# A decoder layer on one core: the second MLP product begins with four column tiles taken together, and units of its first chunk are loaded and split later

## The chip, the cores and the metric

The kernel runs on one core of one Trainium2 chip. The metric is the device time of one execution in microseconds (us); lower is better. Three runs of the kernel before are shown, and one more execution was taken with the hardware profiler. All stretches and times below are microseconds from the start of the profiled span.

## What is computed

One layer of a hybrid decoder on a residual stream of 512 positions and 2048 columns, in float32. The change touches only the MLP of the layer:

```
f = jnp.square(jax.nn.relu(rms_norm(h, norm_mlp_pre[i]) @ mlp_w1[i])) @ mlp_w2[i]
h = h + rms_norm(f, norm_mlp_post[i])
```

`mlp_w1` is 2048 by 8192 and `mlp_w2` is 8192 by 2048. Ahead of the MLP stand the recurrent and attention mixers and their output product, behind it a gate product with `ple_gate`.

## The kernel before

**Split products.** Every float32 operand is split into a rounded part (hi) and what is left (lo). ScalarE writes hi (line 155), VectorE writes lo from the source and hi (line 156), and one 128x128 weight block times one activation tile is three matmuls into the same PSUM bank (`mm3`, lines 163 to 165): hi with hi, hi with lo, lo with hi. A split activation tile of 128 contraction rows is a *unit* (hi and lo side by side). Units lie in two rings of buffers, `cx` with 14 and `cy` with 10.

**Strips.** The program of the second half of the layer is a list of *strips*. A strip is a piece of weights of 128 by 512, four blocks of 128x128, so it gives 12 matmuls. `go` walks the list; step j does three things in this order: it issues the work hooked to step j, it splits the weights of strip j+4, and it issues the matmuls of strip j, with the work hooked to the quarters of the step between them. `at(j, ...)` hooks work to a step (quarters are allowed). There are five buffers for split strips (tags `shi` and `slo`), so the split of strip j+4 waits until TensorE is through strip j-1. All orders are fixed by the numbers of the hooks; each engine and the DMA queue of SyncE take their instructions strictly in that order, and wait only where data or a buffer is missing.

**The first MLP product** (`mlp_w1`) ends in pairs of column tiles, each worked out with seven products instead of eight (`pair_a`, `add_pair`). A pair has 14 strips, and its matmuls have 256 columns of activations. Sums of weights for it lie in a ring of three buffers (tag `wsum`, 128x1024 each); the last pair holds two of the three, one until its tenth strip is split and one until its fourteenth. Weights as they arrive lie in a ring of five buffers (tag `raw`, 128x1024). The squared result goes to a DRAM tensor `f_d`.

**The second MLP product** (`mlp_w2`, in `back`, from the line `base = len(self.strips)`) is cut into 4 chunks of 16 units (2048 contraction rows each); every chunk goes over 16 column tiles, 4 strips each (`add_full`), and its matmuls have 512 columns. For each chunk, `load_f` (line 1506) brings two tiles of `f_d` at a time, 512 KB, into one `wsum` buffer, and `prep_b` splits one of them into a unit. For the first chunk, the loads and the splits are hooked to steps ahead of the first strip, `base`:

```
o = F0 + 0.5 * k if c == 0 else F1 + 4 * k if k < 8 else F2 + 0.4 * (k - 8)
if k % 2 == 0:
    at(cb + o - (4 if c == 0 or k < 14 else 0.5), load_f, c, k)
at(cb + o, prep_b, c, k)
```

With F0 = -11.75 the first load is hooked 15.75 steps ahead of the product, one more follows with every step, and the 16 splits are hooked from step base-11.75 to base-4.25, two to a step. The last pair of the first product is strips base-14 to base-1.

`add_plain` (line 242), which two other products of the layer use already, orders strips otherwise: it takes up to four column tiles together. Its first step issues the first strips of all four columns, block by block (for each block of 128 rows, the four columns in turn, 48 matmuls); then come the second strips of the four columns, the third and the fourth. Each column has a PSUM bank of its own.

Of the kernel before, what the change touches and what calls it, by code (L numbers as in the profile page):

```python
# [18 lines left out]
KT = D // P  # L19
# [11 lines left out]
FC = 16  # L31
NCHUNK = DFF // P // FC
FW = 10
F0, F1, F2 = -11.75, -48, -3
NTAB = 1039
H = S // 2
PRIO = 20000
# [1 line left out]
RMT = 11.5  # L39
WO = (-12, -11, -10, -9, -7, -5)  # L40
NPL = 6
NPG = 6
G6 = (-7, -6)
G4 = 21
# [91 lines left out]
class Build:  # L136
# [32 lines left out]
    def at(self, j, fn, *a):  # L169
        key = math.floor(4 * j + 0.5)  # L170
        assert self.now is None or key > self.now, (key, self.now)
        self.hooks.setdefault(key, []).append((fn, a))
# [1215 lines left out]
    def back(self):  # L1388
        nc, A, T, at = self.nc, self.A, self.T, self.at
# [55 lines left out]
        def plain_a(m0):  # L1445
            def f(i, ps, st):
                if i % 2 == 0:
                    st["z"] = x_tile()
                t = st["z"][:, i % 2]
                v.tensor_tensor(t, ps, T["Rm"], op=ALU.mult)  # L1450
                v.scalar_tensor_tensor(t, t, 0.0, t, op0=ALU.max, op1=ALU.mult)
                if i % 2:
                    self.store(self.f_d[m0 + i - 1:m0 + i + 1].rearrange("a p n -> p a n"), st["z"])
            return f

        def sink_a(m):
            def f(p, ps, st):
                z = self.z_evict(p, ps, st)
                if z is not None:
                    zf = z.rearrange("p a n -> p (a n)")  # L1460
                    v.scalar_tensor_tensor(zf, zf, 0.0, zf, op0=ALU.max, op1=ALU.mult)
                    self.store(self.f_d[m:m + 2].rearrange("a p n -> p a n"), z)
            return f
# [13 lines left out]
        self.add_plain(bk, [A["mlp_w1"][m] for m in range(4)], up, plain_a(0), "Rm", (-8.5, -7.5, -6.5, -5.5))  # L1477
        if NPL > 4:
            self.add_plain(bk + 16, [A["mlp_w1"][m] for m in range(4, NPL)], up, plain_a(4), "Rm", (-7, -6))
        for k in range(KT):  # L1480
# [9 lines left out]
        b = len(self.strips)  # L1490
        for m in range(NPL, DFF // P, 2):
            self.pair_a(b, A["mlp_w1"], m, ua, sink_a(m), first=m == NPL and NPL == 4, offs=WO if m == NPL and NPL > 4 else None, last=m == DFF // P - 2)
            b += 14
# [8 lines left out]
        ub = [[] for _ in range(NCHUNK)]  # L1502
# [15 lines left out]
        def out_b(c, m, ps):  # L1518
            y = self.y_row(m)
            if c == 0:  # L1520
                act.activation(y, ps, AF.Copy)
            else:
                v.tensor_tensor(y, ps, y, op=ALU.add)
            if c == NCHUNK - 1:
                sq = self.msum if m == 0 else self.sum_tile("fsq")[:, :S]
                act.activation(sq, y, AF.Square)  # L1526
                if m >= KT - 2:
                    sq_last.append(sq)
                elif m:
                    g.tensor_tensor(self.msum, self.msum, sq, op=ALU.add)  # L1530

        def add_full(c, m):
            q, st = {}, []
            b = len(self.strips)

            def load(h):
                q[h] = self.raw_tile()
                nc.sync.dma_start(q[h], A["mlp_w2"][c, m][:, h * 1024:(h + 1) * 1024])

            def mm(s):  # L1540
                def f(j, k):
                    if s + k == 0:
                        st.append(self.bank())
                    hi, lo = self.hl[j]
                    u = ub[c][4 * s + k]
                    self.mm3(st[0], hi[:, k * P:(k + 1) * P], lo[:, k * P:(k + 1) * P], u[:, 0], u[:, 1],
                             s + k == 0, s == 3 and k == 3)
                    if s == 3 and k == 3:
                        self.wait.append(("j", out_b, c, m, st[0]))
                return f  # L1550

            for h in range(2):
                at(b + 2 * h - FW, load, h)
            for s in range(4):
                self.strips.append(Strip(lambda s=s: q[s // 2][:, (s % 2) * 512:(s % 2 + 1) * 512], mm(s)))

# [2 lines left out]
        for c in range(NCHUNK):  # L1559
            cb = len(self.strips)  # L1560
            for k in range(FC):
                o = F0 + 0.5 * k if c == 0 else F1 + 4 * k if k < 8 else F2 + 0.4 * (k - 8)
                if k % 2 == 0:
                    at(cb + o - (4 if c == 0 or k < 14 else 0.5), load_f, c, k)
                at(cb + o, prep_b, c, k)
            for m in range(KT):
                add_full(c, m)


        last = len(self.strips)  # L1570
# [42 lines left out]
        def plain_g(i, ps, st, m0=0):  # L1613
            i += m0
            pp, h = T["ph", i - i % 2]
            o = pp[:, i % 2]
            t = T["fb"].tile([P, S], F32, tag="t2", name="og", bufs=1)
            act.activation(t, ps, AF.Sigmoid)
            g.tensor_tensor(o, o, t, op=ALU.mult)  # L1619
            g.tensor_tensor(o, o, h[:, i % 2], op=ALU.add)  # L1620
            if i % 2:
                self.store(self.out[:, i - 1:i + 1, :], pp, GD)

        def g_sink(m):
            def f(p, ps, st):
                z = self.z_evict(p, ps, st)
                if m < KT - 2:
                    parts = [(r, slice(0, S)) for r in range(2)] if z is not None else []
                else:
                    parts = self.done({2: 0, 7: 2}.get(p, p))  # L1630
                if not parts:
                    return
                (pp, h), zz = T["ph", m], st["z"]
                for r, c in parts:
                    o = zz[:, r, c]
                    act.activation(o, o, AF.Sigmoid)
                    v.tensor_tensor(o, o, pp[:, r, c], op=ALU.mult)
                    v.tensor_tensor(o, o, h[:, r, c], op=ALU.add)
                if m < KT - 2:
                    self.store(self.out[:, m:m + 2, :], z, 2)  # L1640
                elif p == 4:
                    nc.sync.dma_start(self.out[:, m + 1, :], zz[:, 1])
                elif p in (2, 3, 7):
                    nc.sync.dma_start(self.out[:, m, c], o)
            return f
# [14 lines left out]
        self.add_plain(bg, [A["ple_gate"][m] for m in range(4)], ug, plain_g, "Rf", (-12, -11, -10, -7))  # L1660
        if NPG > 4:
            self.add_plain(bg + 16, [A["ple_gate"][m] for m in range(4, NPG)], ug,
                           lambda i, ps, st: plain_g(i, ps, st, 4), "Rf", G6)
# [3 lines left out]
        at(bg + GL + 1, load_ph, 2)  # L1667
        for m in range(NPG, KT, 2):
            b = len(self.strips)
            self.pair_a(b, A["ple_gate"], m, ue, g_sink(m), last=m == KT - 2, offs=GO if m == NPG else None,  # L1670
                        lo=lambda p, m=m: g if p in GP and m == NPG else None)
            at(b + GH, load_ph, m)
# [99 lines left out]
```

## Time and profile before

| | |
|---|---|
| median of 3 runs | 2459.36 us (2458.16 to 2459.91) |
| the profiled execution | 2458.5 us, of which the span is 2456.7 us |
| instructions | 34978 |
| TensorE busy | 2342.9 us, 95% of the span |
| VectorE, ScalarE, GpSimd busy | 1544.3, 1076.8, 243.5 us |
| granted TensorE clock, mean | 0.979 |

In the profile, PE is TensorE's matmuls, DVE VectorE, ACT ScalarE, and SPq the DMA queue of SyncE. A row of a timeline begins with the start and the duration; what stands in brackets at its end is the idle time of that engine just before, and what ended it. A matmul's duration reaches past the start of the next one, so the spacing of starts is what it costs in a row of matmuls. Names lose their digits: `in_mlp_w_dram` is either of the two weight tensors.

### The profile page before, as it was taken

To read this page: it belongs to the slowest core of one execution; us is meant where nothing else is said; L and a number is where in the kernel's file an instruction comes from. 1 tells how busy PE (TensorE), PEld (TensorE's weight loads), DVE (VectorE), ACT (ScalarE), POOL (GpSimd) and SP (SyncE) were. 2 spreads that over 40 slices of the span, in tenths; PEclk is the share of its full clock that TensorE was granted. 3 is DMA by queue.
4 is the path that set the end of the run, shared out by engine and by line. 5 is a ranking of instruction groups with operands and counts; after the bars stand their busy time and mean duration, and the time that the engine had idled before them with its cause. 6 is when DMAs were issued, how large, how long until landed. Compare 5 with 4: busy or idle time off the path is not lost.

```text
span 2456.7 us, 34978 instructions
## 1 busy us (share of the span) xinstructions
PE 2342.9 (95%) x13178; PEld 2046.3 (83%) x13178; DVE 1544.3 (63%) x2543; ACT 1076.8 (44%) x2008; POOL 243.5 (10%) x238
## 2 busy tenths in 40 slices
PE   7999999989999778999999998999999999997899
PEld 6788888777788658999999997888888888886688
DVE  6364755588746789888888886333333333335898
ACT  5354655478733445444444444333223223223454
POOL 4000000134400440000000000000000000112420
PEclk9999999999999889999999999999999999998999
DMA  5452232422234532343433333434333333233644
GB/s 191 159 180 93 99 108 97 133 89 84 82 129 164 191 103 98 127 138 130 136 131 134 134 135 126 159 116 133 112 112 137 121 103 131 101 112 128 223 142 138
DMA packets 114093, 316.75 MB, mean 129 GB/s; under 512 B 11298, under 2 KB 16674, under 8 KB 113924
## 3 DMA queue, kind: packets, MB, share of 16 engines
q1 hardware_dynamic: 94708, 275.13, 34.0%
q10 hardware_dynamic: 19216, 39.39, 4.2%
q8 instruction: 103, 1.69, 0.3%
q14 instruction: 66, 0.54, 0.1%
HBM read 270.37 MB, written 44.11 MB: 128 GB/s over the span
## 4 chain that ended last, share of the span: by engine, by line
PE 62%; DVE 6%; issue 2%; DMA 1%; ACT 1%; POOL 0%; ACTq 0%; DVEq 0%; SPq 0%; POOLq 0%
PE ps_mm L165 20%; PE ps_mm L163 20%; PE ps_mm L164 20%; DVE slo L156 1%; DVE cx L156 1%; DMA fk<-f_d 1%; DVE y L1592 1%; PE ps_t L487 0%; DVE y L442 0%; POOL pz L1619 0%; ACT shi L155 0%; DVE y L1422 0%; DVE cy L156 0%; DVE y L1588 0%; DMA pz<-pp_d 0%
## 5 line engine op out<-in xcount | busy, mean ns | idle before, releaser
L156 DVE TENSOR_TENSOR slo<-raw,shi 128x512 fp32r<-128x512 f32 x802 | 580.0, 729 | 743.1 <-ACT shi L155 727.4
L155 ACT ACTIVATE shi<-raw 128x512 fp32r<-128x512 f32 x804 | 502.2, 629 | 870.5 <-PE ps_mm L164 748.4
L163 PE MATMUL ps_mm<-cx,shi 128*128 128x512 f32 (+1 forms) x2044 | 707.7, 346 | 25.4 <-ACT shi L155 19.8
L164 PE MATMUL ps_mm<-cx,shi 128*128 128x512 f32 (+1 forms) x2044 | 702.1, 343 | 15.0 <-DVE cx L1428 7.5
L165 PE MATMUL ps_mm<-cx,slo 128*128 128x512 f32 (+1 forms) x2044 | 704.0, 344 | 13.0 <-DVE slo L156 10.7
L165 PE MATMUL ps_mm<-cy,slo 128*128 128x512 f32 (+1 forms) x1604 | 555.0, 346 | 6.4 <-DVE slo L156 6.4
L163 PE MATMUL ps_mm<-cy,shi 128*128 128x512 f32 (+1 forms) x1604 | 555.4, 346 | 3.7 <-ACT shi L155 2.0
L164 PE MATMUL ps_mm<-cy,shi 128*128 128x512 f32 (+1 forms) x1604 | 554.9, 346 | 4.1 <-DVE cy L1428 4.1
L163 PEld LDWEIGHTS ps_mm<-cx,shi 128*128 128x128 f32 x2044 | 393.0, 192 | 70.8 <-ACT shi L155 23.5
L165 PEld LDWEIGHTS ps_mm<-cx,slo 128*128 128x128 f32 x2044 | 392.5, 192 | 62.7 <-DVE slo L156 16.6
L164 PEld LDWEIGHTS ps_mm<-cx,shi 128*128 128x128 f32 x2044 | 393.3, 192 | 57.8 <-DVE cx L1428 8.8
L165 PEld LDWEIGHTS ps_mm<-cy,slo 128*128 128x128 f32 x1604 | 305.8, 191 | 44.6 <-DVE slo L156 8.0
L163 PEld LDWEIGHTS ps_mm<-cy,shi 128*128 128x128 f32 x1604 | 305.9, 191 | 40.8 <-ACT shi L155 2.6
L164 PEld LDWEIGHTS ps_mm<-cy,shi 128*128 128x128 f32 x1604 | 305.9, 191 | 40.5 <-DVE cy L1428 4.8
L155 ACT ACTIVATE shi<-wsum 128x512 fp32r<-128x512 f32 x204 | 126.5, 628 | 163.9 <-PE ps_mm L164 87.8
L156 DVE TENSOR_TENSOR slo<-wsum,shi 128x512 fp32r<-128x512 f32 x204 | 138.7, 687 | 44.8 <-ACT shi L155 44.8
L1530 POOL TENSOR_TENSOR msum<-msum,fsq 128x512 f32<-128x512 f32 x13 | 16.9, 1297 | 1288.7 <-ACT fsq L1526 1288.7
L1257 POOL TENSOR_SCALAR al_P<-al_P,ar_sts 128x512 f32<-128x512 f32 (+3 forms) x128 | 74.2, 601 | 63.8 <-ACT al_ph L1279 29.3
L163 PE MATMUL ps_mm<-y,shi 128*128 128x256 f32 x272 | 76.4, 281 | 1.2 <-ACT shi L155 1.2
L1247 ACT ACTIVATE al_P<-al_P,ar_stm 128x512 f32<-128x512 f32 (+3 forms) x128 | 70.4, 554 | 16.1 <-DVE ar_stm L1242 15.8
L165 PE MATMUL ps_mm<-y,slo 128*128 128x256 f32 x272 | 76.1, 280 | 0.8 <-DVE slo L156 0.8
L164 PE MATMUL ps_mm<-y,shi 128*128 128x256 f32 x272 | 75.9, 279 | 0.0
(356 smaller groups left out, 2336.3 us busy)
## 6 DMA issues: line engine op xcount, KB each, us to landing
raw<-in_mlp_w_dram SPq DMA_DIRECT2D x254, 512.0 KB, 3.7
raw<-in_w_in_dram SPq DMA_DIRECT2D x64, 512.0 KB, 3.5
raw<-in_w_out_dram SPq DMA_DIRECT2D x32, 512.0 KB, 3.5
fk<-f_d SPq DMA_DIRECT2D x32, 512.0 KB, 5.0
raw<-in_ple_gate_dram SPq DMA_DIRECT2D x32, 512.0 KB, 4.8
f_d<-z ACTq DMA_DIRECT2D x29, 512.0 KB, 2.8
y<-in_xT_dram SPq DMA_DIRECT2D x16, 256.0 KB, 6.2
raw<-in_w_v_dram SPq DMA_DIRECT2D x8, 512.0 KB, 4.3
```

The source lines that it names most:

```text
L155: nc.scalar.activation(hi, src, AF.Copy)
L156: (eng or nc.vector).tensor_tensor(lo, src, f32(hi), op=ALU.subtract)
L163: mm(ps, whi, ahi, start=start, stop=False)
L164: mm(ps, whi, alo, start=False, stop=False)
L165: mm(ps, wlo, ahi, start=False, stop=stop)
L1247: act.activation(PP[qt, b], PP[qt, b], AF.Exp, scale=-1.0, bias=st["mn"][:, qt, b:b + 1], accum_out=st["sm"][:, qt, b:b + 1])
L1257: pool.tensor_scalar(PP[qt, b], PP[qt, b], st["sm"][:, qt, b:b + 1], 1.0, op0=ALU.mult, op1=ALU.mult)
L1530: g.tensor_tensor(self.msum, self.msum, sq, op=ALU.add)
L1592: v.scalar_tensor_tensor(y, y, V[:, V_MLPPOST + k:V_MLPPOST + k + 1], T["h"][k], op0=ALU.mult, op1=ALU.add)
```

## The change

The first four column tiles of the first chunk go through `add_plain` instead of `add_full`. Their first weight loads are hooked to steps base-12 to base-9. The times of the loads and splits of the first chunk's 16 units come from two tables, `CL` (8 loads) and `CU` (16 splits): loads from base-10 to base+5.25, splits from base-6 to base+8.5. The two columns behind the four load their weights 8 steps ahead instead of 10. Nothing else is changed; the arithmetic and the number of matmuls, splits and transfers are the same.

```
-F0, F1, F2 = -11.75, -48, -3
+F1, F2 = -48, -3
...
+CU = (-6, -4.75, -3.5, -2.25, -1, -0.5, 0.25, 0.75, 4.25, 4.75, 5.25, 5.75, 7, 7.5, 8, 8.5)
+CL = (-10, -7.5, -5, -2.75, 0.25, 0.75, 1.75, 5.25)
...
-        def add_full(c, m):
+        def add_full(c, m, lead):
...
-                at(b + 2 * h - FW, load, h)
+                at(b + 2 * h - lead, load, h)
...
-                o = F0 + 0.5 * k if c == 0 else F1 + 4 * k if k < 8 else F2 + 0.4 * (k - 8)
+                o = CU[k] if c == 0 else F1 + 4 * k if k < 8 else F2 + 0.4 * (k - 8)
                 if k % 2 == 0:
-                    at(cb + o - (4 if c == 0 or k < 14 else 0.5), load_f, c, k)
+                    at(cb + CL[k // 2] if c == 0 else cb + o - (4 if k < 14 else 0.5), load_f, c, k)
                 at(cb + o, prep_b, c, k)
-            for m in range(KT):
-                add_full(c, m)
+            if c == 0:
+                self.add_plain(cb, [A["mlp_w2"][c, m] for m in range(4)], ub[c], lambda i, ps, st: out_b(0, i, ps), "j",
+                               (-12, -11, -10, -9))
+            for m in range(4 if c == 0 else 0, KT):
+                add_full(c, m, 8 if c == 0 and m < 6 else FW)
```

The queue of SyncE, around the start of the second product. First before; `raw` of line 307 is the last pair's weights, `fk` the loads of `f_d`, `raw` of line 1538 the new product's weights:

```order
L307 DMA raw<-in_mlp_w_dram 128x1024 x116
L1506 DMA fk<-f_d 128x2x512 x6
L1538 DMA raw<-in_mlp_w_dram 128x1024
L1506 DMA fk<-f_d 128x2x512 x2
L1538 DMA raw<-in_mlp_w_dram 128x1024 x11
```

And with the change (line numbers are 2 higher; line 248 is the load of `add_plain`):

```order
L309 DMA raw<-in_mlp_w_dram 128x1024 x116
L248 DMA raw<-in_mlp_w_dram 128x1024 x2
L1508 DMA fk<-f_d 128x2x512
L248 DMA raw<-in_mlp_w_dram 128x1024 x2
L1508 DMA fk<-f_d 128x2x512 x2
L248 DMA raw<-in_mlp_w_dram 128x1024
L1508 DMA fk<-f_d 128x2x512 x3
L248 DMA raw<-in_mlp_w_dram 128x1024
L1508 DMA fk<-f_d 128x2x512
L248 DMA raw<-in_mlp_w_dram 128x1024 x2
L1508 DMA fk<-f_d 128x2x512
L1540 DMA raw<-in_mlp_w_dram 128x1024 x3
```

Six loads of `f_d` stood ahead of the first weight load of the new product; now four weight loads stand among the first two of `f_d`, and the others follow one to three at a time.

ScalarE at the end of the last pair. `shi` is the hi part of a strip, `cx` and `cy` that of a unit. Before, from the split of strip base-8 on:

```order
L155 ACTIVATE shi<-raw 128x512
L155 ACTIVATE cx<-fk 128x512 x2
L155 ACTIVATE shi<-raw 128x512
L155 ACTIVATE cx<-fk 128x512 x2
L155 ACTIVATE shi<-wsum 128x512
L384 ACTIVATE snp_15530<-ps_mm 128x256
L155 ACTIVATE cy<-fk 128x512 x2
L155 ACTIVATE shi<-wsum 128x512
L155 ACTIVATE cy<-fk 128x512 x2
L155 ACTIVATE shi<-raw 128x512
L155 ACTIVATE cy<-fk 128x512 x2
```

With the change, from the splits of strips base-4 and base-3 on:

```order
L157 ACTIVATE shi<-raw 128x512 x2
L157 ACTIVATE cx<-fk 128x512
L157 ACTIVATE shi<-wsum 128x512 x2
L157 ACTIVATE cx<-fk 128x512
L157 ACTIVATE shi<-raw 128x512
L157 ACTIVATE cx<-fk 128x512
L157 ACTIVATE shi<-raw 128x512
L157 ACTIVATE cx<-fk 128x512
L157 ACTIVATE shi<-raw 128x512
L157 ACTIVATE cy<-fk 128x512
L157 ACTIVATE shi<-raw 128x512
L157 ACTIVATE cy<-fk 128x512
```

Two units stood between any two strips of the last pair; now all strips of the pair but two are split ahead of the first unit, and from the second unit on one stands between two strips.

## Rows read from the trace of the kernel before

**Rows 1.** The page's first part, busy time of each engine.
```profile
PE 2342.9 (95%) x13178; PEld 2046.3 (83%) x13178; DVE 1544.3 (63%) x2543; ACT 1076.8 (44%) x2008; POOL 243.5 (10%) x238
```
**Rows 2.** Stretches: length, busy of PE, PEld, DVE, ACT, POOL, granted clock, DMA, GB/s.
```profile
1499.74:1511.27 11.53, 11.53 (x98) 11.48 (x96) 7.52 (x12) 3.35 (x6) 0.00 (x0) 1.00 0.28 92
1511.27:1537.48 26.21, 14.07 (x74) 11.70 (x73) 14.57 (x24) 12.01 (x23) 0.00 (x0) 0.80 0.51 173
1600.00:1650.00 50.00, 50.00 (x222) 41.44 (x221) 15.49 (x23) 16.88 (x29) 0.00 (x0) 1.00 0.35 116
```
**Rows 3.** Timeline of TensorE, end of the last pair and first matmuls of the new product.
```profile
1511.15 0.28 PE L165 MATMUL ps_mm<-cx,slo 128*128 128x256 f32 x1
1513.22 0.39 PE L163 MATMUL ps_mm<-cx,shi 128*128 128x256 f32 x1 [1.80 <-ACT shi L155]
...
1518.69 0.39 PE L163 MATMUL ps_mm<-cx,shi 128*128 128x256 f32 x1 [3.12 <-ACT shi L155]
...
1520.72 0.58 PE L165 MATMUL ps_mm<-cx,slo 128*128 128x256 f32 x1 [1.52 <-DVE slo L156]
...
1525.62 0.58 PE L163 MATMUL ps_mm<-cx,shi 128*128 128x256 f32 x1 [2.40 <-ACT shi L155]
...
1537.48 0.50 PE L163 MATMUL ps_mm<-cx,shi 128*128 128x512 f32 x1 [0.80 <-ACT shi L155]
1537.82 0.40 PE L164 MATMUL ps_mm<-cx,shi 128*128 128x512 f32 x1
1538.37 0.50 PE L165 MATMUL ps_mm<-cx,slo 128*128 128x512 f32 x1 [0.16 <-DVE slo L156]
1538.71 0.39 PE L163 MATMUL ps_mm<-cx,shi 128*128 128x512 f32 x1
```
**Rows 4.** Timeline of ScalarE, the second pair of units and the strip behind it.
```profile
1511.50 1.15 ACT L155 ACTIVATE cx<-fk 128x512 fp32r<-128x512 f32 x2 [4.09 <-DMA fk<-f_d]
1512.56 0.61 ACT L155 ACTIVATE shi<-wsum 128x512 fp32r<-128x512 f32 x1
```
**Rows 5.** The chain that ended last, one round trip: start, length, what.
```profile
1507.89 3.59 DMA fk<-f_d
1511.50 0.64 ACT cx L155
...
1513.49 3.46 DMA fk<-f_d
```
**Rows 6.** Waits of SyncE's DMA queue, 1480 to 1570: total, times, longest.
```profile
SPq L1506 <- DVE cx L156: 12.2, 2, 10.2
SPq L1506 <- DVE cy L156: 7.9, 4, 3.1
```
**Rows 7.** Loads of units and weights between 1485 and 1560, and from issue to landing.
```profile
raw<-in_mlp_w_dram SPq DMA_DIRECT2D x13, 512.0 KB, 4.7
fk<-f_d SPq DMA_DIRECT2D x8, 512.0 KB, 3.8
```
**Rows 8.** The tile of unit loads over the whole program.
```profile
DMA to landing us min/median/max: 3.5/5.0/6.4
```
**Rows 9.** Costliest groups of the page: splits of strips, mean ns after the busy time.
```profile
L156 DVE TENSOR_TENSOR slo<-raw,shi 128x512 fp32r<-128x512 f32 x802 | 580.0, 729 | 743.1 <-ACT shi L155 727.4
L155 ACT ACTIVATE shi<-raw 128x512 fp32r<-128x512 f32 x804 | 502.2, 629 | 870.5 <-PE ps_mm L164 748.4
```
**Rows 10.** Timeline of TensorE in the gate product's first block, also in the order of `add_plain`.
```profile
2265.39 0.63 PE L163 MATMUL ps_mm<-cx,shi 128*128 128x512 f32 x1
2265.82 0.63 PE L164 MATMUL ps_mm<-cx,shi 128*128 128x512 f32 x1
...
2268.22 0.39 PE L163 MATMUL ps_mm<-cx,shi 128*128 128x512 f32 x1
...
2272.99 0.39 PE L163 MATMUL ps_mm<-cx,shi 128*128 128x512 f32 x1
```
**Rows 11.** Stretches of that block, columns as in group 2.
```profile
2260.00:2270.00 10.00, 8.19 (x25) 6.57 (x26) 7.99 (x12) 3.54 (x7) 0.61 (x1) 0.65 0.58 190
2270.00:2280.00 10.00, 10.00 (x45) 8.26 (x45) 4.94 (x8) 2.79 (x5) 0.00 (x0) 1.00 0.91 327
```

## The prediction

> **What bounds the kernel now.** First the page's busy times: TensorE is busy for 2342.9 of 2456.7 us [rows 1], so no other engine is the bound over the whole, and what can be gained is TensorE's idle time and its time at half clock. Then the stretches around the change. In the eight strips up to 1511.27 TensorE is never idle and at full clock; in the 26.21 us up to 1537.48 it is busy for 14.07 us at a mean clock of 0.80; later in the second product it is busy for 50.00 of 50 us at clock 1.00 [rows 2]. So the second product itself has nothing to give, and the join of the two products has.
>
> The timeline of TensorE says what the join loses. The last matmul in full step starts at 1511.15; then there are gaps of 1.80, 3.12, 1.52 and 2.40 us and smaller ones, most of them ended by ScalarE's hi part of a strip [rows 3]. ScalarE is not short of time. It sat idle for 4.09 us until a load of `f_d` landed, wrote two units, and only then the strip that TensorE wanted, at 1512.56 [rows 4]. The strip stood behind the units in ScalarE's order, and the units behind a load.
>
> Why the loads are late is seen in the queue: loads of `f_d` waited 12.2 and 7.9 us for VectorE to finish a unit, not for an engine to move data [rows 6]. Two of the three `wsum` buffers still belong to the last pair, so the early loads go one after the other through the third: load, hi, lo, next load. One such round trip takes 1513.49 - 1507.89 = 5.60 us, 3.59 of it the transfer [rows 5]; the program asks for two units per step, and a step of the pair lasts 11.53 / 8 = 1.44 us [rows 2].
>
> **The sum.** *Removed: the wait ahead of the product.* From 1511.27 on, six strips of the pair are left, 72 matmuls. At 1.44 us a strip they need 8.65 us, so the product could begin at 1519.92; it begins at 1537.48 [rows 3]. That is 17.56 us, half clock included.
>
> *Removed: small waits in the first strip.* Its first three spacings take 1538.71 - 1537.48 = 1.23 us [rows 3]. Three full ones are 3 x 0.227 = 0.68 us, from 21 spacings between 2268.22 and 2272.99 [rows 10]. Another 0.55 us.
>
> *Moved: the 16 units and 8 loads.* They all remain: 16 hi parts of about 0.63 us and 16 lo parts of about 0.69 us (the two-unit row in [rows 4] and the strips' groups in [rows 9] agree to a few hundredths). They cost nothing only if TensorE has split strips and units in time, so I follow the program's new order from step to step, with step base-n at 1519.92 - 1.44n.
>
> All strips of the pair but the last two are now split before the first unit, so their slack of four steps stays. The first load takes the third buffer, which is free, and stands in the queue only behind weights whose buffers the pair gives back as it starts; it is out some six steps before its first unit is wanted. The second load takes the buffer of the pair's first sum, free once strip base-5 is split (about 1510), lands after 3.8 us [rows 7] at 1514, and is wanted by ScalarE at 1514.8, behind strip base. The tight one is the third load. Its buffer is that of the pair's other sum, free after strip base-1 is split: that waits for TensorE to reach step base-5 (1512.7), then 0.63 and 0.69 us [rows 9], so the load is issued at 1514.1 and lands at 1517.9. Unit 4 is then ready (hi) at 1518.5. Behind it in ScalarE's order stands the first strip of the fourth column, ready at 1519.2; its lo part, behind three evictions of PSUM and unit 4 on VectorE, at about 1520.7. TensorE wants that strip at its tenth matmul, 1519.92 + 9 x 0.227 = 1521.96, and the lo part at 1522.4. So it is in time by 1.7 us.
>
> From there the block helps itself. Its first step is 48 matmuls on units 0 to 3 alone, 10.9 us, to 1530.8. Units 4 to 7 are wanted then, 8 to 11 at 1541.7, 12 to 15 at 1552.6. From the fourth load on, each reuses the buffer of the load three before it, so transfers overlap with splits; loads 4 and 5 are out by 1518, the eighth by about 1533. In the block the strip splits wait for TensorE: the second strip of the second column can be split only when matmul 38 of the 48 frees its buffer (1528.5), is wanted at 1533.5, and nothing that waits for a load stands in front of it: unit 7 is done by then.
>
> *The bound of that step.* Below, it is nothing: it cannot give back more than the two sums above. Above, I take the slowest landing of any `f_d` load in the program, 6.4 us [rows 8]: the third load lands at 1520.5, the hi part is ready at 1521.8, the lo part at 1522.5, late by 0.1 us. I take 0 and keep 0.1, and 2 us more for what a hand-followed order can miss.
>
> *Added: four column tiles at once.* TensorE changes the PSUM bank every three matmuls. In the gate product, which has this order already, the spacing within such a block is 0.227 us at full clock [rows 10, 11]. So 0. The Trainium skill, in TensorE: Matmul & The Clock Gate, section Loop structure matters more than you think, shows as the good order all K tiles of one output tile before the next, and as the bad one a wait in front of every matmul that turns the clock down. The change leaves that good order for 16 strips; the rows at 2268 to 2273 show that the order alone does no harm, and what a wait would do is a rival below.
>
> *Moved: weight loads.* Four now stand among the first two loads of `f_d`. In this stretch weight loads landed after 4.7 us, loads of `f_d` after 3.8 [rows 7]; at 4.7 the third load lands at 1518.8 and is still in time. The next two columns' loads are hooked later, but are wanted 16 strips after base. 0.
>
> **Sum:** 17.56 + 0.55 = 18.1 us off the profiled execution's 2458.5 us, 2440.4 us. That execution stands 0.86 us below the median of the runs, so the median comes out at 2459.36 - 18.1 = **2441.3 us**. What follows the join is full TensorE time, so nothing there can swallow the gain.
>
> **Rivals.** *The third load is caught behind weight loads.* The load of the first column's second half is issued right after it, and two of the others just before. The Trainium skill, in DMA: Bandwidth & Descriptors, section Queues, rings and completion order, says that each DMA engine takes the descriptors of one queue's ring in order; all these loads go through SyncE's queue. By that rule the third load waits out whatever weights are unfinished ahead of it. For: weights need 4.7 us [rows 7]. Against: those ahead of it are issued four microseconds or more before. If it landed after 10 us, at 1524.1, the fourth column would be ready 3.5 us late, about as long as the 3.12 us gap after which the slow rows begin (1520.72 and beyond, [rows 3]); with some 9 us at half clock behind it, 4.5 us more, that gives 2449.
>
> *The loads still go one at a time.* This is the change not doing what it says. Round trips of 5.60 us from 1507 on would bring units 4 and 5 at about 1524, the fourth column 3 to 5 us late, then half clock: about 2451. Against: from the fourth load on three buffers are in turn.
>
> *Slower: the block runs at half clock.* If the first block starts with a gap like that of 3.12 us [rows 3] and then meets another at every strip, TensorE stays at the lower of its two levels, 1.2 instead of 2.4 GHz, as it did at 2265 in the gate product: spacing 0.43 [rows 10], mean clock 0.65 in that stretch [rows 11]. Over the 192 matmuls of the four columns that is 192 x (0.43 - 0.227) = 39 us, so 2441 + 39 = 2480. For: the gate product does begin so. Against: there each unit comes out of a norm that has only just ended, and the block was back at full clock by 2268; here four units are ready at the start. It decides if unit 3 or the fourth column's strip is as late as that, and units 8 to 15 after it too.
>
> **How the numbers follow.** The forecast 0.87, weights ahead 0.05, one at a time 0.04, half clock 0.03, and 0.01 for a part of the wait that stays for no reason I see and leaves under 4.9 us. A difference of 0.2%, 4.9 us, is about what a measurement of this kernel can tell from none. The first three cases are beyond that on the fast side: faster 0.96, same 0.01, slower 0.03. The forecast's own spread is 2440 to 2444 (run to run a little under 1 us either way, 0.1 to 2 us of missed waits); I take the range from 2439.5 to 2446, toward the two rivals above it.
>
> **What would show it.** Right: the product's first matmul of 512 columns about 8.6 us after the one that now starts at 1511.15, no gap over 1 us between, granted clock 1.00 from 1500 to 1600; ScalarE's idle time ended by TensorE, not by `f_d`. Wrong: gaps of TensorE in the first block ended by the hi part of a strip or by a unit, loads of `f_d` that land after 6 us or more, or queue waits on VectorE's units as long as now.

## The result, and the profile after

The changed kernel takes 2440.24 us (median of 4 runs, 2439.23 to 2440.52), the kernel before, on the same chip, 2459.64 us (4 runs, 2458.16 to 2461.43). The ratio is 0.992, 95% interval 0.9903 to 0.9937: 19.4 us less, where 18.1 were forecast, and inside the range of 2439.5 to 2446 us. The profiled executions differ by 2456.7 - 2438.7 = 18.0 us of span.

The page's first part of the kernel after, which answers to [rows 1]: the busy time of TensorE falls by 7.0 us, 5.5 of them in the six strips of the join, which ran in part at half clock before (14.07 us busy in [rows 2], 8.59 below); the other engines do about the same work as before.

```profile
PE 2335.9 (96%) x13178; PEld 2041.1 (84%) x13178; DVE 1542.4 (63%) x2543; ACT 1076.9 (44%) x2008; POOL 242.6 (10%) x238
```

Stretches of the kernel after, with the columns of [rows 2]: the eight strips ahead, the last six strips of the pair, the 48 matmuls of the new block's first step, and a later stretch.

```profile
1499.24:1510.79 11.55, 11.55 (x99) 11.55 (x98) 10.31 (x17) 5.44 (x10) 0.00 (x0) 1.00 0.60 205
1510.79:1519.38 8.59, 8.59 (x75) 8.59 (x73) 7.98 (x15) 6.12 (x11) 0.00 (x0) 1.00 0.78 267
1519.38:1530.28 10.90, 10.90 (x50) 9.01 (x49) 6.10 (x10) 3.89 (x7) 0.00 (x0) 1.00 0.72 250
1600.00:1650.00 50.00, 50.00 (x223) 41.39 (x222) 14.87 (x22) 15.47 (x27) 0.00 (x0) 1.00 0.31 107
```

The six strips that took 26.21 us at a mean clock of 0.80 [rows 2] now take 8.59 us at 1.00, without idle time. The DMA engines pay for it with a share of 0.78 in those 8.59 us, where it was 0.51 before.

The timeline of TensorE after, where [rows 3] had six rows with idle time. No row between 1500 and 1580 has any; the first matmul of 512 columns starts at 1519.38, and the tenth, the fourth column's first, at 1521.45.

```profile
1510.79 0.28 PE L165 MATMUL ps_mm<-cx,shi 128*128 128x256 f32 x1
...
1519.38 0.40 PE L165 MATMUL ps_mm<-cx,shi 128*128 128x512 f32 x1
1519.62 0.39 PE L166 MATMUL ps_mm<-cx,shi 128*128 128x512 f32 x1
...
1521.45 0.39 PE L165 MATMUL ps_mm<-cx,shi 128*128 128x512 f32 x1
```

The timeline of ScalarE after, which answers to [rows 4].

```profile
1504.22 0.63 ACT L157 ACTIVATE shi<-wsum 128x512 fp32r<-128x512 f32 x1 [4.19 <-PE ps_mm L167]
...
1514.63 0.63 ACT L157 ACTIVATE cx<-fk 128x512 fp32r<-128x512 f32 x1 [0.25 <-DMA fk<-f_d]
...
1518.03 0.63 ACT L157 ACTIVATE cy<-fk 128x512 fp32r<-128x512 f32 x1 [0.77 <-DMA fk<-f_d]
1518.56 0.61 ACT L157 ACTIVATE shi<-raw 128x512 fp32r<-128x512 f32 x1
...
1522.01 0.63 ACT L157 ACTIVATE cy<-fk 128x512 fp32r<-128x512 f32 x1 [1.79 <-DMA fk<-f_d]
...
1528.29 2.66 ACT L157 ACTIVATE shi<-raw 128x512 fp32r<-128x512 f32 x4 [5.12 <-PE ps_mm L166]
```

ScalarE still waits for loads of `f_d`, 2.8 us in three waits, but no strip behind those waits comes late for TensorE. 1518.03 is unit 4, of the third load; 1518.56 is the fourth column's first strip, split 2.9 us before TensorE takes it up at 1521.45. The row at 1528.29 is the strip splits of the block, now held by TensorE itself.

The waits of SyncE's queue after, 1480 to 1570 (total, times, longest), which answer to [rows 6]: the waits for units are 4.9 us where they were 20.1, and 4.4 us are waits for the pair's sums (`slo`), as the prediction's order of buffers had it.

```profile
SPq L1508 <- DVE slo L158: 4.4, 3, 3.8
...
SPq L1508 <- DVE cy L158: 2.9, 2, 2.1
SPq L1508 <- DVE cx L158: 2.0, 1, 2.0
```

One thing got slower: the loads of `f_d` between 1490 and 1560 now take 5.4 us to land, and up to 7.2, where 3.8 was the median before [rows 7].

```profile
DMA to landing us min/median/max: 3.8/5.4/7.2
```

**Two stretches that can be compared in every trace.** The ScalarE row with a wait of 4.19 us for TensorE (1504.22 above) is the split of the same strip of the last pair in all traces; the last sum of the norm behind the MLP, a row of the tile `ps_t`, ends the second product. From the mark to the first matmul of 512 columns is the *join*, from there to the norm's last sum is the *product*. The row of the norm in the kernel after (first and last start behind the durations):

```profile
L489 PE MATMUL ps_t<-ones,msum x48: 164/250/372, 38.0 to 2223.2; 128*128 128x1 f32 x48
```

So the join is 1519.38 - 1504.22 = 15.16 us and the product 2223.2 - 1519.38 = 703.8. The same rows of the other traces give the table below, where "lost" is join and product together against the kernel after. Medians are of the runs of each kernel. They scatter more than the table: the mark itself, with nearly the same program ahead of it, comes between 1498.70 us (e8) and 1505.40 (e4) in the ten traces, so a loss of a few us is read from the stretches.

| kernel | join | product | lost | median us |
|---|---|---|---|---|
| before | 32.78 | 704.4 | 18.2 | 2459.64 |
| after | 15.16 | 703.8 | 0 | 2440.24 |
| e1_order_only | 33.42 | 705.9 | 20.4 | 2460.87 |
| e2_late_only | 15.16 | 707.7 | 3.9 | 2443.15 |
| e3_extra_buffers | 22.30 | 704.0 | 7.3 | 2448.79 |
| e4_weights_late | 15.16 | 709.8 | 6.0 | 2445.05 |
| e5_one_buffer | 15.16 | 714.0 | 10.2 | 2449.51 |
| e6_units_ahead | 15.16 | 704.0 | 0.2 | 2440.80 |
| e7_third_late | 15.16 | 705.4 | 1.6 | 2441.74 |
| e8_third_later | 15.16 | 711.2 | 7.4 | 2446.23 |

### The profile page after: what moved, and what is told of

Read it like the earlier page. It is cut to its first block, busy times and chain, and to the rows that moved or that the text cites. A ratio compares the mean times of both kernels' runs of the same rounds, so it can differ in the third digit from the quotient of the medians.

```text
span 2438.7 us, 34976 instructions
## 1 busy us (share of the span) xinstructions
PE 2335.9 (96%) x13178; PEld 2041.1 (84%) x13178; DVE 1542.4 (63%) x2543; ACT 1076.9 (44%) x2008; POOL 242.6 (10%) x238
## 4 chain that ended last, share of the span: by engine, by line
PE 63%; DVE 5%; issue 2%; ACT 1%; DMA 1%; POOL 0%; ACTq 0%; DVEq 0%; POOLq 0%; SPq 0%
PE ps_mm L167 21%; PE ps_mm L165 21%; PE ps_mm L166 21%; DVE slo L158 1%; DVE cx L158 1%; DVE y L1597 1%; PE ps_t L489 0%; DVE y L444 0%; ACT shi L157 0%; POOL pz L1624 0%; DVE y L1424 0%; DVE y L1593 0%; DVE cy L158 0%; DMA raw<-in_ple_gate_dram 0%; DMA raw<-in_mlp_w_dram 0%
```

## The experiments

The change has three parts: the order of the columns, the later units and loads, the place of the weight loads. **Theory A**: the gain is that ScalarE no longer waits for single-buffered loads of units ahead of strips that TensorE wants. **B**: the order of the columns itself brings it. **C**: the earlier place of the weight loads brings it. The first four kernels shared 13 runs of the kernel before (median 2459.31 us, 2454.15 to 2462.65), the last four 10 (2460.67 us, 2452.49 to 2462.33).

### e1: the order of the columns alone

```
-                o = CU[k] if c == 0 else F1 + 4 * k if k < 8 else F2 + 0.4 * (k - 8)
+                o = -11.75 + 0.5 * k if c == 0 else F1 + 4 * k if k < 8 else F2 + 0.4 * (k - 8)
...
-                    at(cb + CL[k // 2] if c == 0 else cb + o - (4 if k < 14 else 0.5), load_f, c, k)
+                    at(cb + o - (4 if c == 0 or k < 14 else 0.5), load_f, c, k)
```

> The four column tiles together, with the loads and splits of the units at their old steps. Theory A (the time was lost in single-buffer round trips of the loads of f_d, standing ahead of the strips in ScalarE's order): the round trips are all back, the join loses its 17 us again, 2455 to 2460 us. Theory B (what helps is the order of the columns, since units 4 to 15 are wanted later): nearly all of the gain is there, 2441 to 2447 us.

Measured: 2460.87 us (10 runs, 2457.0 to 2463.66), ratio 1.0005, interval 0.9996 to 1.0015: no gain, and 0.9 us above the range that A gave. The gaps of TensorE are back, each within 0.1 us of its old length:

```profile
1509.04 0.39 PE L165 MATMUL ps_mm<-cx,shi 128*128 128x256 f32 x1 [1.86 <-ACT shi L157]
...
1514.53 0.39 PE L165 MATMUL ps_mm<-cx,shi 128*128 128x256 f32 x1 [3.15 <-ACT shi L157]
...
1516.55 0.58 PE L167 MATMUL ps_mm<-cx,slo 128*128 128x256 f32 x1 [1.45 <-DVE slo L158]
...
1521.43 0.58 PE L165 MATMUL ps_mm<-cx,shi 128*128 128x256 f32 x1 [2.38 <-ACT shi L157]
```

1.86, 3.15, 1.45 and 2.38 us stand where the kernel before had 1.80, 3.12, 1.52 and 2.40 [rows 3]. B falls as the whole cause: with the units at their old steps, the order of the columns and the earlier weight loads bring nothing. What they bring once the units are late is not shown here.

### e2: the later units alone

The kernel before, with one number changed; loads and splits keep their spacing and come 5.75 steps later.

```
-F0, F1, F2 = -11.75, -48, -3
+F0, F1, F2 = -6, -48, -3
```

> The kernel before with one number changed: the units of the first chunk are split from step base-6 on, two per step, the loads four steps ahead of them, and the columns one by one as before. Theory A: each load finds a buffer given back by the pair or by an earlier unit, strips of the pair stand ahead of the units, and unit 15 is ready at about the time the fourth strip wants it; 2440 to 2446 us. Theory B: with one column at a time units 4 to 15 are wanted in the first four strips, so the late units stall the product instead; 2452 us or more.

Measured: 2443.15 us (4 runs, 2440.89 to 2447.17), ratio 0.9934, interval 0.9918 to 0.9951. The join is 15.16 us, as in the kernel after: one number removes the whole wait ahead of the product. What is left is in the product's first strips. Its first 48 matmuls take 1533.49 - 1518.75 = 14.74 us, where the block of the kernel after takes 10.90; these 3.8 us are the 3.9 us of the table. The first of them, the longest of their waits and the row behind the last, in the timeline of TensorE:

```profile
1518.75 0.40 PE L163 MATMUL ps_mm<-cx,shi 128*128 128x512 f32 x1
...
1529.91 0.50 PE L164 MATMUL ps_mm<-cy,shi 128*128 128x512 f32 x1 [1.23 <-DVE cy L156]
...
1533.49 0.39 PE L163 MATMUL ps_mm<-cx,shi 128*128 128x512 f32 x1
```

TensorE now waits for a unit. One column after the other wants all 16 units within 10.9 us; four columns at once want four. VectorE, which writes the lo parts, has no time left for that: in the columns of [rows 2] it is busy for 11.97 of the 12.00 us up to 1533.50, where it was busy for 6.10 of 10.90 in the block of the kernel after. The unit of the longest wait stood there behind a row of 1.22 us for the pair's results (tile `z`, from 1528.03).

```profile
1521.50:1533.50 12.00, 10.13 (x38) 6.41 (x38) 11.97 (x22) 8.30 (x16) 0.00 (x0) 1.00 0.92 331
```

So 3.9 us in the traces, 2443.15 - 2440.24 = 2.9 in the medians (whose intervals overlap), is what this kernel still lacks. It differs from the kernel after in the order of the columns, in the steps of the units and in the weight loads; that the order is what brings the 3.9 us is argued from the 16 units and the four, and no run has it alone with late units.

### e3: more buffers instead of later steps

The kernel before, with four of the first chunk's eight loads in a buffer for two that stands idle there, so that early loads need not take turns through one.

```
+            if c == 0 and k in (0, 2, 10, 12):
+                if k in (0, 10):
+                    T["fkx"] = T["fb"].tile([P, 2, 2, S], F32, tag="fy", name="fkx", bufs=1)
+                t = T["fkx"][:, (k // 2) % 5]
+            else:
+                t = self.sum_tile("fk").rearrange("p (a n) -> p a n", a=2)
```

> The kernel before with every hook as it was, but four of the eight loads of f_d go into a buffer of two tiles that is idle until the gate product. Theory A: fewer loads wait for a unit, so most of the waits ahead of the product go, with some left where a load still waits for a buffer of the pair; 2442 to 2450 us, first gaps later than 1511. Theory B, and any theory in which the order of the columns or the splits' number per step decides: no change, 2457 to 2461 us.

Measured: 2448.79 us (4 runs, 2448.3 to 2449.82), ratio 0.9957, interval 0.9942 to 0.9971. Most of the gaps are gone; one long one is left, shown first as ScalarE's wait:

```profile
1517.27 1.15 ACT L155 ACTIVATE cy<-fk 128x512 fp32r<-128x512 f32 x2 [6.08 <-DMA fk<-f_d]
```

and then as TensorE's, with the slow rows behind it:

```profile
1518.99 0.39 PE L163 MATMUL ps_mm<-cx,shi 128*128 128x256 f32 x1 [3.55 <-ACT shi L155]
...
1519.88 0.58 PE L165 MATMUL ps_mm<-cx,slo 128*128 128x256 f32 x1 [0.38 <-DVE slo L156]
```

ScalarE waits here for units 6 and 7, the fourth load. The expectation had such a wait at a buffer of the pair; SyncE's queue shows another one, its longest in this stretch:

```profile
SPq L1511 <- DVE cy L156: 16.2, 2, 14.3
```

The load stood until VectorE had written units 4 and 5 out of the third load's buffer: one round trip that the added buffers leave. Order and steps are those of the kernel before; only buffers were added, and 10.5 us of 19.4 came. So the round trips through one buffer are shown as the cause of the waits, as A has it.

### e4: the weight loads back to later steps

The kernel after, with the four columns' first weight loads 5 steps later.

```
-                               (-12, -11, -10, -9))
+                               (-7, -6, -5, -4))
```

> The changed kernel with the four columns' first weight loads hooked at base-7 to base-4 instead of base-12 to base-9, so that two of them follow the third load of f_d in the queue. Theory A: the third and fourth column's weights land about when their strips are split; 0 to 2 us lost, 2440 to 2443 us. Theory C (the weight loads put ahead in the queue are what removed the wait): several strips late and the clock at half level again, 2447 us or more.

Measured: 2445.05 us, 4 runs from 2438.51 to 2449.62, ratio 0.9939, interval 0.9917 to 0.996: between the theories, and spread over 11 us. The profiled execution is one of the two long ones (2448.51 us). ScalarE waits for the third column's weights:

```profile
1523.33 0.63 ACT L157 ACTIVATE shi<-raw 128x512 fp32r<-128x512 f32 x1 [4.91 <-DMA raw<-in_mlp_w_dram]
```

TensorE stands for 1.90 us and then turns slow:

```profile
1524.01 0.50 PE L165 MATMUL ps_mm<-cx,shi 128*128 128x512 f32 x1 [1.90 <-ACT shi L157]
...
1525.88 0.63 PE L166 MATMUL ps_mm<-cx,shi 128*128 128x512 f32 x1
```

The stretch of that wait, then the one behind it; the two last columns are DMA share and GB/s:

```profile
1520.00:1524.00 4.00, 2.12 (x13) 1.50 (x11) 0.01 (x1) 0.67 (x2) 0.00 (x0) 1.00 1.03 361
1524.00:1530.00 6.00, 5.57 (x12) 3.58 (x13) 5.97 (x11) 3.30 (x6) 0.00 (x0) 0.53 0.61 205
```

The DMA engines are busy all the time there. SyncE issued three weight loads from 1515.36 on, in the midst of loads of `f_d`; the waited-for one landed at 1523.3, and the load of `f_d` issued right behind them, at 1516.87, took 10.6 us, the longest of them between 1490 and 1560. The Trainium skill, in DMA: Bandwidth & Descriptors, section Queues, rings and completion order, has each DMA engine take one queue's descriptors in order. These numbers agree with that, since the load landed 4 us after the waited-for weights ahead of it; with a share of 1.03 full engines alone may delay it too, and no run tells the two apart. So C holds in part: the early weight loads bring no gain of their own (e1), but in the profiled execution 6.0 us are lost without them. What the faster runs of this kernel did is not known, since they have no trace.

### e5: all unit loads through one buffer

The kernel after, with the first chunk's eight loads through a single idle buffer.

```
+            if c == 0:
+                t = T["fb"].tile([P, 2, 2, S], F32, tag="fy", name="fkx", bufs=1)[:, 0]
+            else:
+                t = self.sum_tile("fk").rearrange("p (a n) -> p a n", a=2)
```

> The changed kernel, but all eight loads of the first chunk's units go through one buffer (an idle one of the same size), so that each waits for both units of the load before it, and nothing of the pair's is waited for. Theory A (round trips of single-buffered loads are what delays strips; the rotation of three buffers is needed from the third load on): round trips of about 5.6 us, units 4 and 5 land near 1524, the fourth column's first strip comes 3 to 5 us late, then some half clock: 2445 to 2452 us, likeliest 2448. Rival (only the late hooks and the column order matter, the buffers do not): 2440 to 2442 us, and no idle row of TensorE over 1 us in the first block.

Measured: 2449.51 us (6 runs, 2441.77 to 2453.61), ratio 0.9955, interval 0.9937 to 0.9972. A is met. Unit 4 comes 5.46 us after the product's start, where the kernel after has it 1.35 us ahead. ScalarE:

```profile
1522.76 0.63 ACT L157 ACTIVATE cy<-fkx 128x512 fp32r<-128x512 f32 x1 [3.94 <-DMA fkx<-f_d]
...
1543.24 0.63 ACT L157 ACTIVATE shi<-raw 128x512 fp32r<-128x512 f32 x1 [5.93 <-DMA raw<-in_mlp_w_dram]
...
1558.49 0.63 ACT L157 ACTIVATE cx<-fkx 128x512 fp32r<-128x512 f32 x1 [4.76 <-DMA fkx<-f_d]
1559.03 0.61 ACT L157 ACTIVATE shi<-raw 128x512 fp32r<-128x512 f32 x1
```

TensorE at the fourth column, followed by rows of half clock up to 1529.25, and its second gap of over 1 us:

```profile
1523.96 0.79 PE L165 MATMUL ps_mm<-cx,shi 128*128 128x512 f32 x1 [3.62 <-ACT shi L157]
...
1559.69 0.50 PE L165 MATMUL ps_mm<-cy,shi 128*128 128x512 f32 x1 [1.67 <-ACT shi L157]
```

Both gaps are of A's kind: the strip that TensorE wants (split at 1523.30 and at 1559.03) stands in ScalarE's order behind a unit whose load is late, of the third load and of the eighth.

The ScalarE row at 1543.24 is of another kind that was not expected: a strip that waits for *weights*. It cost TensorE nothing, which has no idle row between the two gaps, but it shows what SyncE's order does. In SyncE's rows a row's length holds all its issues; three loads of `f_d` fill 1525.35 to 1538.58, each waiting for its buffer. The weight load behind them goes out only then:

```profile
1525.35 13.23 SPq L1511 DMA_DIRECT2D fkx<-f_d  x3
1538.63 0.46 SPq L248 DMA_DIRECT2D raw<-in_mlp_w_dram  x1
```

### e6: two units ahead of the last two strips

```
-CU = (-6, -4.75, -3.5, -2.25, -1, -0.5, 0.25, 0.75, 4.25, 4.75, 5.25, 5.75, 7, 7.5, 8, 8.5)
+CU = (-6, -4.75, -3.5, -2.25, -2, -1.75, 0.25, 0.75, 4.25, 4.75, 5.25, 5.75, 7, 7.5, 8, 8.5)
```

> The changed kernel, but units 4 and 5 are hooked a step earlier, so that ScalarE splits them, and waits for their load, ahead of the first strips of the third and fourth columns. The load lands at about 1517.9. Theory A with the prediction's slack: the third column's strip is ready near 1520, wanted at 1521.3, the fourth's near 1521, wanted at 1522: no gap over 0.5 us, 2440 to 2442 us. If the slack is smaller than worked out: gaps of 1 to 3 us ended by the hi part of those strips, and 2442 to 2447 us. Rival (it is the count of units between strips and not their load that costs): no difference either way, 2440 to 2441.

Measured: 2440.80 us (4 runs, 2439.01 to 2442.94), ratio 0.9924, interval 0.9904 to 0.9944, no different from the kernel after. The product starts at 1520.05 here. ScalarE waits for the third load with both strips behind the wait (1518.84 is the third column's, 1519.89 the fourth's):

```profile
1518.31 0.63 ACT L157 ACTIVATE cy<-fk 128x512 fp32r<-128x512 f32 x1 [1.29 <-DMA fk<-f_d]
1518.84 0.62 ACT L157 ACTIVATE shi<-raw 128x512 fp32r<-128x512 f32 x1
1519.37 0.62 ACT L157 ACTIVATE cy<-fk 128x512 fp32r<-128x512 f32 x1
1519.89 1.14 ACT L157 ACTIVATE shi<-raw 128x512 fp32r<-128x512 f32 x2
```

TensorE has no idle row from 1500 to 1570. So a wait in front of strips costs nothing while the strips stay ahead of their matmuls. A and its rival both allow this result; it shows only that the slack is there.

### e7 and e8: the third load 3.3 and 6.6 us later

The load of units 4 and 5 is made once more into the same buffer in e7, twice more in e8 (`range(2 ...)`); the units wait for the last.

```
+            for _ in range(1 if (c, k) == (0, 4) else 0):
+                nc.sync.dma_start(t, self.f_d[c * FC + k:c * FC + k + 2].rearrange("a p n -> p a n"))
```

> The changed kernel, with the third load of units made twice into the same buffer, 512 KB more; units 4 and 5 wait for the second landing, about 4 us later. Theory A (a margin of 1.7 us in this load): the fourth column's first strip is late by about 2 us, one gap of TensorE of 1.5 to 3 us near 1522 ended by that strip, no lasting half clock: 2442 to 2444 us. Rival (the first block has more slack than worked out, or the queue lets the two overlap): 2440 to 2441 us, no gap.

> The changed kernel, with the third load of units made three times into the same buffer; units 4 and 5 wait for the third landing, about 8 us later. Theory A: the fourth column's first strip is late by about 6 us and the clock falls behind the gap: 6 us and some 3 to 5 us of half clock, 2447 to 2452 us. Rival (gaps alone cost, the clock does not fall): 2445 to 2447 us.

Measured for e7: 2441.74 us (4 runs, 2439.37 to 2444.69), ratio 0.9928, interval 0.9908 to 0.9948. That is between the two ranges, and by its median alone it could not be told from the kernel after; the trace tells it. Unit 4 comes 1521.33 - 1518.03 = 3.30 us later (both products start within 0.01 us), and the fourth column's strip with it, in ScalarE's rows:

```profile
1521.33 0.63 ACT L157 ACTIVATE cy<-fk 128x512 fp32r<-128x512 f32 x1 [4.08 <-DMA fk<-f_d]
1521.87 0.61 ACT L157 ACTIVATE shi<-raw 128x512 fp32r<-128x512 f32 x1
```

TensorE's one gap in this stretch stands at that strip; the granted clock from 1520 to 1540 is 1.00.

```profile
1522.54 0.50 PE L165 MATMUL ps_mm<-cx,shi 128*128 128x512 f32 x1 [0.93 <-ACT shi L157]
```

The matmul starts 0.67 us after its strip's hi part does (1521.87), so in the kernel after, with the hi part at 1518.56, it could have started at 1519.23; it starts at 1521.45. The slack is 2.22 us. 3.30 - 2.22 = 1.08 us, and 1522.54 - 1521.45 = 1.09. A had a gap of 1.5 to 3 us from a margin of 1.7; the kind is right, the size was too high. The other 0.5 us of the table's 1.6 are shorter delays right behind the gap.

Measured for e8: 2446.23 us (5 runs, 2443.99 to 2447.29), ratio 0.9945, interval 0.9928 to 0.9962. The profiled execution is the lowest of the five: it came to the join 5.5 us earlier than the kernel after did (product at 1513.86). Unit 4 comes at 1519.13, 5.27 us after the product's start instead of 1.35 us ahead of it: 6.62 us later. Less the slack that is 4.40 us, and the fourth column's matmul starts 4.40 us after its place (1513.86 + 2.07 = 1515.93). ScalarE's row of unit 4:

```profile
1519.13 0.63 ACT L157 ACTIVATE cy<-fk 128x512 fp32r<-128x512 f32 x1 [7.38 <-DMA fk<-f_d]
```

and TensorE's:

```profile
1520.33 0.79 PE L165 MATMUL ps_mm<-cx,shi 128*128 128x512 f32 x1 [4.23 <-ACT shi L157]
1520.92 0.63 PE L166 MATMUL ps_mm<-cx,shi 128*128 128x512 f32 x1
...
1526.74 0.40 PE L165 MATMUL ps_mm<-cx,shi 128*128 128x512 f32 x1
```

Fifteen matmuls then take 1526.74 - 1520.33 = 6.41 us instead of 3.41, at a granted clock of 0.52, so half clock adds 3.0. 4.4 + 3.0 = 7.4 us, the table's loss. The median lies 0.8 us under the range that A gave and inside that of the rival, but the rival said that the clock does not fall, and it does: A was right in kind and too high in size, since the two extra loads take 6.6 us and not 8.

No variant has a lower median than the changed kernel, which has nothing left to gain at this place: no idle row of TensorE and full clock from 1500 to 1580.

## Why the prediction was right

**What bounds the kernel.** Right, and shown by e1 to e3: later units alone (e2) remove the wait ahead of the product, buffers alone (e3) most of it, the columns' order alone (e1) none. The wait was ScalarE's order together with round trips of one buffer, not ScalarE's speed. The transfer is 3.59 us of a round trip's 5.60 [rows 5]; it counted because the loads went one at a time.

**Removed: the wait ahead of the product, 17.56 us.** Measured 32.78 - 15.16 = 17.62 us between the same two rows.

**Removed: small waits in the first strip, 0.55 us.** Measured 704.4 - 703.8 = 0.6 us over the whole product, which also bears out "nothing there can swallow the gain". The sum of the traces is 18.2 us, the spans differ by 18.0, the forecast was 18.1. That the medians differ by 19.4 is inside their interval (0.9903 to 0.9937 is 15.5 to 23.9 us). The prediction took the spread of runs as a little under 1 us either way, from three runs; the 13 and 10 later runs of the kernel before span 8.5 and 9.8 us. So that the median came within 1.1 us of the forecast is partly luck; the two stretches of the trace are not.

**Moved: 16 units and 8 loads, 0.** Right. The third load, the tight one, was followed by hand to an issue at 1514.1, unit 4 ready at 1518.5 and the fourth column's lo part at 1520.7; the trace has that unit's hi part from 1518.03 to 1518.66 and the lo part ready at 1520.2. The margin of the lo part was given as 1.7 us: it is 1521.91 - 1520.18 = 1.73. That of the hi part, 2.22 us by e7, was not far from the 2.8 that the text implies (1521.96 - 1519.2).

**The bound of that step, 0.1 us.** Too small, though nothing came of it. It rested on 6.4 us as the slowest landing of an `f_d` load; in the kernel after the fourth load took 7.2, in e4 one took 10.6. The trace of before could not show them, since there the loads stood one at a time; the change makes transfers fall together, with a DMA share of 0.78. Had the third load taken 7.2, it would have cost about what e7 shows, 1 to 2 us; that is an estimate, no run shows it.

**Added: four column tiles at once, 0.** Right in the price of the order: 48 matmuls in 10.90 us are 0.227 us each. But the order seems to have its worth: with late units and one column at a time e2 loses 3.9 us to units that come late, and the 0 for the moved units rests on the late times at which the new order wants them (1530.8, 1541.7 and 1552.6 in the prediction).

**Moved: weight loads, 0.** Right for the change as it is. Its margin was not worked out: in e4 the same loads five steps later cost 6.0 us in the trace and 4.8 in the median of four runs that span 11 us.

**The rivals.** A third load that is caught behind weights did not happen, and e8 prices such a delay. The prediction had 8 us for a load 6.2 us late (1524.1 instead of 1517.9), 3.5 of lateness and 4.5 of half clock; e8 has 7.4 us for one 6.6 us late, 4.4 and 3.0. Loads one at a time was e5: forecast about 2451, measured 2449.51, though part of its loss came at the eighth load and not at the place that was named. A first block at half clock was not seen: after 4.40 us of delay in e8 the clock was back within 6.4 us, and no second gap followed. Its condition, a gap at every strip, came in no run, so its price stays untested.

**The signs that were named.** The first matmul of 512 columns came 8.59 us after the start of the pair's last six strips (1510.79), without a gap and at clock 1.00, as forecast. ScalarE's idle time is not ended by TensorE alone, 2.8 us still are by `f_d`. And one sign of "wrong" did appear, a load of `f_d` that took over 6 us (7.2): it was the fourth load, whose units were not wanted yet.

## What to carry to other kernels

An engine that takes its work in order can hold up the busiest one while it has much idle time itself: look at what stands ahead of the late instruction in its order, and move *that* later, to where its data can be there. When loads share a few buffers with work that is about to end, ask when each buffer comes free and hook the load to that point, since a load hooked earlier only blocks the queue for all behind it (in e5 three such loads stood ahead of a weight load for 13 us). Here, once the wait was gone, transfers fell together and landed later, 5.4 us where it was 3.8; a margin taken from landing times of before was too narrow.

## What was not expected

- Loads of 512 KB that landed in 3.8 us while they went one at a time took 5.4 us (up to 7.2) at a DMA share of 0.72 to 0.78 and 250 to 267 GB/s, and one of 10.6 us in e4 spans the stretch at 361 GB/s and a share of 1.03. The runs of e4 lie up to 11 us apart (2438.51 to 2449.62), where those of the kernel after lie within 1.3; but the kernel before has runs 8.5 us apart, so how much of that is the four loads' place in the queue stays open.
- With one column at a time and late units (e2) VectorE was full, 11.97 of 12.00 us, although it is busy for 63% of the span over the whole program.
- The length of a gap alone did not tell whether the clock falls. Gaps of 0.93 us (e7) and 1.23 us (e2) left it at full speed, ones of 1.80 us in the kernel before [rows 3] and 1.86 us in e1 did too, one of 1.90 us in e4 was followed by slow rows within a microsecond. Behind gaps of 3.62 us (e5) and 4.23 us (e8) the slow rows lasted 5.3 and 6.4 us. What decides between them stays open.
